# Gated DeltaNet and routed experts on one core: modulation moved to TensorE, the triangular inverse in blocks of 16 rows, and a planner with other durations

## The chip, the core and the metric

The kernel runs on one core of a Trainium2 chip. The metric is the time of one execution on the device in microseconds (us). Five engines work side by side, each in the fixed order of its own queue: TensorE (PE in the profile, its weight loads PEld), VectorE (DVE), ScalarE (ACT), GpSimd (POOL) and SyncE (SP), which here does nothing but issue DMAs. An instruction that waits holds up all that stands behind it on its engine.

## The reference, cut to what matters

One layer of depth, 512 latent tokens and 256 context tokens of width 1024. First the six modulation vectors (`mod`), a normalised and modulated input, the bidirectional gated DeltaNet with 8 heads of 128, then 16 experts of which each takes 64 tokens.

```python
mod = c_act @ w_mod[i] + b_mod[i]            # 1024 -> 6 * 1024: sh_m, sc_m, gt_m, sh_f, sc_f, gt_f
u = modulate(rmsnorm(h, norm_mix_g[i]), sh_m, sc_m)
...
# in gated_deltanet, for each direction, head and chunk
a_low = where(strict, einsum('bhnid,bhnjd->bhnij', k_beta, k) * decay, 0.0)
lmat = a_low + eye(CHUNK)
sol = triangular_solve(lmat, rhs, lower=True, unit_diagonal=True)
...
def step(S, inp):                            # scan over chunks
    v_new = u_n - w_n @ S
    o_n = qd_n @ S + att_n @ v_new
    S = S * gt_n + kt_n.T @ v_new
...
h = h + gt_m * y
h = h + gt_f * ec_moe(modulate(rmsnorm(h, norm_ffn_g[i]), sh_f, sc_f), ...)
```

## The kernel before, in words

**Two stages.** The first is the token mixer: norms, modulation, projections, eight heads, output projection, router. The second runs the 16 experts and reads some 400 MB of expert weights through a ring of buffers; its first weights are fetched (`prefetch`, `fetch`) while the mixer ends.

**The mixer per head.** `bulk` (L400 on) projects v, q, k and z with the split input (`proj_step`, L141 to L143: three matmuls a step, eight steps an item, 31 items in all, those of k and v also for the context). `conv` runs the short convolution on DVE and ACT. Then each head goes through:
- `head_a` (L1050 on): decay matrices `ff`, read by a broadcasting DMA from `grow_d` and masked on POOL; k times k on PE (L1114); the product `ct`, of which the diagonal blocks go into `cd` and by DMA to `bd` in DRAM.
- `invert` (L1130 on): `lb` is read back so that 96 partitions hold 48 blocks of 32 rows, each twice, for the even and the odd columns of the inverse. POOL then works forward substitution, 31 steps of a product (`tb`, L1148) and a subtraction (`xb`, L1150). The result goes out to `xd` and comes back as `cr`.
- `head_b` (L1208 on): the blocks of 32 are merged to 64 and to 128 on PE, with copies and transposes on DVE and ACT between, into `XT`.
- `scan` (L1304 on): both directions over 6 chunks, each with a chain of PE, DVE, PE, ACT, PE, DVE; needs `XT` and the scan of the head before. `head_o` (L1358 on) normalises the output, which the tail multiplies with the output weights (L457 to L459).

**The modulation for later.** `mods` (L337 on) loads 32 pieces of the modulation weights, 128 columns each, into two slots (`e<-in_wm`). `mod_piece` weights each of the 8 slabs of 128 rows with the activation and adds them: on DVE in 8 steps (L373, L375), or on POOL or ACT with a tree of additions, by a letter for each piece in the table `MOD_E`. One small matmul with ones then sums over partitions (L382, L396), and DVE adds it into its place.

**What sets the order.** All five queues of the mixer come from a planner inside the program (`run`, L205 on). Each step is written as a generator that asks for an engine and a duration (`Ask("P", 0.67, ...)`); the planner plays them against a clock of its own with ranks (scans first, projections last), a delay `HOP` after each engine, a model of the DMA (`dma`), and rings of buffers, and the instructions are written in the order in which steps start there. On the chip the queues keep that order; only the waits are real. Names with a trailing number are tiles of the heads (`ck`, `cv`, `e`, `ua`, `wa`, `ya` hold k, v, XT and others in turn).

Of the kernel before, what the change touches and what calls it, by code (L numbers as in the profile page):

```python
# [11 lines left out]
F32 = mybir.dt.float32  # L12
F32R = mybir.dt.float32r
AF = mybir.ActivationFunctionType
OP = mybir.AluOpType
# [4 lines left out]
P = 128  # L20
D = 1024
# [18 lines left out]
NB = 2 * NCH * 4  # L40
# [9 lines left out]
def gdn_moe_kernel(ctx: ExitStack, tc: tile.TileContext, a, out):  # L50
# [3 lines left out]
    def psum_tile(pool, shape, tag, bufs, name=None):  # L54
# [9 lines left out]
    par = const.tile([2 * NB, 2], F32)  # L64
    g.affine_select(out=par[:, 0:1], in_=ones[:2 * NB, 0:1], pattern=[[0, 1]], compare_op=OP.is_ge, fill=0.0,
                    base=NB - 1, channel_multiplier=-1)
    g.affine_select(out=par[:, 1:2], in_=ones[:2 * NB, 0:1], pattern=[[0, 1]], compare_op=OP.is_ge, fill=0.0,
                    base=-NB, channel_multiplier=1)
# [7 lines left out]
    v.tensor_add(selr, selr, ident[:, 96:])  # L76
    epsc = const.tile([P, 3], F32)
# [71 lines left out]
    HOP = {"P": 0.27, "A": 0.33, "V": 0.33, "G": 0.35, "D": 0.0, None: 0.0}  # L149
    PRE = 1  # L150
    E_AT = (410, 425)
    EARLY_G = 4
    MOD_STEP = 7
    MOD_E = "GGAGVVVVGVBVAVAVVVVVAVGAVVVVBVGV"
# [5 lines left out]
    def dma(nbytes, at=0.0):  # L160

        dq[0] = max(dq[0], at + 0.7) + nbytes / 360e3
        return dq[0] + 1.1
# [75 lines left out]
    av = lambda n_: 0.1 + n_ * 0.00084  # L239
    dv = lambda n_: 0.08 + n_ * 0.00104  # L240
# [17 lines left out]
    def conv(nm, h, n_, parts, last):  # L258
# [8 lines left out]
        else:  # L267
# [10 lines left out]
            for j in range(5):  # L278
                t = yield Ask("VA"[j == 0], 1.06 * dv(w) if j else 1.11 * av(w), t)
                if j == 0:  # L280
                    s.mul(t_, pad[:, o:o + w], taps[:, 0:1])
                else:
                    v.scalar_tensor_tensor(t_, pad[:, o + j:o + j + w], taps[:, j:j + 1], t_, op0=OP.mult, op1=OP.add)
# [63 lines left out]
    def mod_piece(n_, j, wm, wsl, t):  # L347

        t = yield Ask(None, 0.0, lambda: t if n_ < 2 else None if ("mm", n_ - 2) not in done else max(t, done["mm", n_ - 2]))
        if MOD_E[n_] != "V":  # L350
            if MOD_E[n_] == "G":
                for i in range(2):
                    t = yield Ask("G", 1.25, t)
                    hk = slice(4 * i, 4 * i + 4)
                    g.tensor_tensor(wm[:, hk], wm[:, hk], cs1[:, hk, 0:1].to_broadcast([P, 4, P]), OP.mult)
            else:
                for i in range(4):
                    t = yield Ask("A", 0.59, t)
                    for k in (2 * i, 2 * i + 1):
                        s.mul(wm[:, k], wm[:, k], cs1[:, k, 0:1])  # L360
            en, on = ("V", v) if MOD_E[n_] == "B" else ("G", g)
            for i in (4, 2):
                t = yield Ask(en, dv(P * i) if en == "V" else 0.25 + 0.27 * i, t)
                on.tensor_add(wm[:, :i], wm[:, :i], wm[:, i:2 * i])
            t = yield Ask(en, dv(P) if en == "V" else 0.5, t)
            acc = accs[n_ % 2]
            on.tensor_add(acc, wm[:, 0], wm[:, 1])
        else:
            acc = accs[n_ % 2]
            for k in range(KT):  # L370
                t = yield Ask("V", 0.25, t)
                if k == 0:
                    v.tensor_scalar(acc, wm[:, k], cs1[:, k, 0:1], None, op0=OP.mult)  # L373
                else:
                    v.scalar_tensor_tensor(acc, wm[:, k], cs1[:, k, 0:1], acc, op0=OP.mult, op1=OP.add)  # L375
        give(wsl, t + 1.0)
        b1 = slice(16 + j, 17 + j)
        t = yield Ask("P", 0.15, t + 3.0, "pq")
        sl = take("pq")
        if 8 <= j < 24:  # L380
            pc = psum_tile(ps, [P, 1], "pq", 3)
            pe.matmul(pc, acc, ones[:, 0:1], start=True, stop=True)  # L382
            k1 = slice(j % 8, j % 8 + 1)
            t = yield Ask("V", 0.15, t)
# [1366 lines left out]
```

## Time and profile before

| | us |
|---|---|
| median of 3 runs | 1574.02 (1568.37 to 1576.02) |
| profiled execution, its own time | 1573.24 |
| its span in the profile | 1571.5 |
| mixer, until the first expert matmuls | 0 to about 634 |
| experts | about 634 to 1571.5 |

Busy times over the span are PE 87%, DVE 46%, ACT 26%, POOL 24%; but the share of an engine that works in one stage alone says little, so the profile is read by stretches. A row of a view of stretches gives the length and then, for each engine, busy time and number of instructions, the granted TensorE clock as a share of full speed, the share of the DMA engines and their GB/s. A busy PE counts the modelled length of overlapping matmuls: what a matmul really takes from the queue is read from the distance between two starts.

### The profile page before, as it was taken

Reading aid. Unit: us, or ns where it says so; the run is one execution under the profiler, and the core shown is the slowest. Engines: PE = TensorE matmul, PEld = TensorE weight load, DVE = VectorE, ACT = ScalarE, POOL = GpSimd, SP = SyncE. Lnnn points to the kernel's source line nnn. Section 1 sums busy time; section 2 is a strip of 40 time slices with the busy share of each in tenths; the row PEclk is TensorE's granted clock in tenths of the full one; section 3 lists DMA queues with packets and bytes.
Section 4 is the critical chain, followed back from the end, with each engine's and each line's share of the span. In section 5 each row is a group of like instructions: output and inputs, shape, how many; then the busy total and the mean of one; then the engine's idle time right before and its main releaser. Section 6 shows DMA issues by size and latency. Waiting matters only on the chain.

```text
span 1571.5 us, 20699 instructions
## 1 busy us (share of the span) xinstructions
PE 1374.7 (87%) x8058; PEld 752.6 (48%) x8058; DVE 721.5 (46%) x1545; ACT 405.3 (26%) x1038; POOL 381.0 (24%) x645
## 2 busy tenths in 40 slices
PE   5889898988986889999999989889889899899867
PEld 1677687766875766433434324224223323324314
DVE  7779896977995896222222222222222222222103
ACT  3356474655574533000000000000000000000012
POOL 2548866857657830000000000000000000000001
PEclk8889999999998999999999999999999999999979
DMA  8145443443453566899999999999999999999992
GB/s 347 54 135 142 135 114 91 117 130 95 133 122 72 205 243 248 364 426 426 425 426 425 425 426 426 427 425 425 426 425 426 426 425 426 425 426 426 425 426 109
DMA packets 112515, 480.12 MB, mean 306 GB/s; under 512 B 45505, under 2 KB 66209, under 8 KB 81826
## 3 DMA queue, kind: packets, MB, share of 16 engines
q1 hardware_dynamic: 112418, 478.81, 77.9%
q8 instruction: 63, 1.03, 0.3%
q14 instruction: 34, 0.28, 0.1%
HBM read 471.92 MB, written 6.86 MB: 305 GB/s over the span
## 4 chain that ended last, share of the span: by engine, by line
DMA 48%; PE 26%; DVE 14%; POOL 8%; issue 2%; ACT 1%; SPq 0%; DVEq 0%; POOLq 0%; ACTq 0%
DMA w<-in_wgu 25%; DMA w<-in_wd 13%; PE gu L1580 10%; PE dn L1561 4%; POOL xb L1150 3%; POOL tb L1148 3%; DMA cr<-xd 2%; DVE e L375 2%; PE gc L1561 2%; PE gc L1511 2%; DMA fg<-in_fg 1%; DVE wl L303 1%; DMA ff__690<-grow_d 1%; DMA ff__1139<-grow_d 1%; PE gc L1548 1%
## 5 line engine op out<-in xcount | busy, mean ns | idle before, releaser
L1580 PE MATMUL gu<-w,xsT 128*64 128x512 f32 x2044 | 472.9, 606 | 32.4 <-DMA w<-in_wgu 31.6
L1580 PEld LDWEIGHTS gu<-w,xsT 128*64 128x64 f32 x2044 | 138.4, 138 | 291.5 <-issue 239.4
L1667 POOL TENSOR_TENSOR hres<-acc,fg 128x256 f32<-128x256 f32 (+1 forms) x6 | 6.0, 1004 | 953.1 <-DVE acc L1655 953.0
L1561 PE MATMUL dn<-w,work 128*64 128x512 f32 x896 | 202.0, 600 | 25.2 <-DMA w<-in_wd 25.2
L1550 DVE TENSOR_TENSOR acc<-gc,acc 128x512 f32<-128x512 f32 x104 | 70.7, 690 | 299.5 <-PE gc L1548 299.5
L141 PE MATMUL pp<-uh,wh 128*128 128x512 f32 (+1 forms) x368 | 153.4, 417 | 1.7 <-ACT cz L265 1.7
L143 PE MATMUL pp<-uh,wl 128*128 128x512 f32 (+1 forms) x368 | 138.9, 377 | 3.8 <-DVE wl L303 2.9
L142 PE MATMUL pp<-ul,wh 128*128 128x512 f32 (+1 forms) x368 | 137.9, 375 | 0.0
L1561 PEld LDWEIGHTS dn<-w,work 128*64 128x64 f32 x896 | 62.4, 137 | 154.2 <-issue 116.8
L1148 POOL TENSOR_TENSOR tb<-lb,xb 96x126 f32<-96x126 f32 (+22 forms) x248 | 118.3, 477 | 65.8 <-DMA lb<-bd 48.6
L1150 POOL TENSOR_TENSOR xb<-xb,tb 96x126 f32<-96x126 f32 (+22 forms) x248 | 125.1, 504 | 19.4
L1532 ACT ACTIVATE work<-tr 128x512 f32<-128x512 f32 x14 | 8.4, 597 | 423.1 <-PE tr L1525 423.1
L1512 DVE TENSOR_SCALAR xsT<-gc,ffn 128x128 f32<-128x128 f32 x64 | 26.2, 410 | 154.1 <-PE gc L1511 154.1
L1542 ACT CAST yh<-work 64x512 fp32r<-64x512 f32 x28 | 17.3, 617 | 253.1 <-DVE work L1539 252.8
L143 PEld LDWEIGHTS pp<-uh,wl 128*128 128x128 f32 x368 | 74.7, 203 | 16.1 <-DVE wl L303 3.3
L141 PEld LDWEIGHTS pp<-uh,wh 128*128 128x128 f32 x368 | 75.1, 204 | 10.7 <-ACT cz L265 2.2
L142 PEld LDWEIGHTS pp<-ul,wh 128*128 128x128 f32 x368 | 75.3, 205 | 6.3
L1511 PEld LDWEIGHTS gc<-oneh,hres 128*128 128x128 f32 x512 | 64.5, 191 | 20.2 <-issue 18.3
L1511 PE MATMUL gc<-oneh,hres 128*128 128x128 f32 x512 | 69.2, 280 | 0.4 <-DVE oneh L1504 0.4
L375 DVE SCALAR_TENSOR_TENSOR e<-e,cs,e 128x128 f32<-128x128 f32 x133 | 66.0, 512 | 1.8
L1613 DVE TENSOR_TENSOR work<-gu,work 128x512 f32<-128x512 f32 x32 | 22.0, 692 | 80.9 <-PE gu L1580 79.7
L1548 PEld LDWEIGHTS gc<-yh,pgt 128*128 128x128 f32 x112 | 19.8, 186 | 82.0 <-issue 68.2
(443 smaller groups left out, 2042.7 us busy)
## 6 DMA issues: line engine op xcount, KB each, us to landing
w<-in_wgu SPq DMA_DIRECT2D x100, 2048.0 KB, 34.3
w<-in_wd SPq DMA_DIRECT2D x45, 2048.0 KB, 34.3
w<-in_wgu SPq DMA_DIRECT2D x55, 1024.0 KB, 31.9
w<-in_wd SPq DMA_DIRECT2D x22, 1024.0 KB, 31.8
e<-in_wm SPq DMA_DIRECT2D x32, 512.0 KB, 4.4
wt<-in_win SPq DMA_DIRECT2D x31, 512.0 KB, 4.6
w<-in_wdt SPq DMA_DIRECT2D x6, 2048.0 KB, 30.7
wm<-in_wm SPq DMA_DIRECT2D x3, 2048.0 KB, 14.6
```

The lines of the kernel that those rows point to most:

```text
L141: pe.matmul(pp, wh[:, k, :], uh[i][:, k, :], start=k == 0, stop=False)
L142: pe.matmul(pp, wh[:, k, :], ul[i][:, k, :], start=False, stop=False)
L143: pe.matmul(pp, wl[:, k, :], uh[i][:, k, :], start=False, stop=k == KT - 1)
L375: v.scalar_tensor_tensor(acc, wm[:, k], cs1[:, k, 0:1], acc, op0=OP.mult, op1=OP.add)
L1148: g.tensor_tensor(t_, lb[:, k + 1:, k:k + 1].to_broadcast([2 * NB, m, n_]), xb[:, k:k + 1, 0:n_].to_broadcast([2 * NB, m, n_]), OP.mult)
L1150: g.tensor_tensor(xb[:, k + 1:, 0:n_], xb[:, k + 1:, 0:n_], t_, OP.subtract)
L1511: pe.matmul(pg, hres[:, t, k * P:k * P + P], oneh[:, t].rearrange("p a b -> p (a b)"), start=t == 0, stop=t == NC_LAT - 1)
L1512: v.tensor_scalar(xsT[:, k, :], pg, ffn[:, 0, k:k + 1], ffn[:, 1, k:k + 1], op0=OP.mult, op1=OP.add)
L1548: pe.matmul(pcb, pgt[:, t, :], yh[:, dh], start=True, stop=True)
L1550: v.tensor_add(acc[t // 2][:, t % 2, cs], pcb, hres[:, t, cs] if first else acc[t // 2][:, t % 2, cs])
L1561: pe.matmul(pd[64 * g_:64 * g_ + 64], hs_[g_][i][:, cb, 64 * j:64 * j + 64], wcols(w, c0, w_), start=ft == 0, stop=ft == 15, tile_position ...
L1580: pe.matmul(gu[m][f // 2][hs], xsT[:, k, es], wcols(w, 2048 * m + 512 * f, 512), start=k == 0, stop=k == KT - 1, tile_position=(0, 64 * (f ...
```

## The change

It has three parts, and the planner then writes all queues of the mixer anew.

1. **Modulation on PE.** `mod_piece` no longer weights and adds on DVE, POOL or ACT, and the table `MOD_E` is gone. Eight matmuls with the activation as 32 columns of weights (`cst`, mostly zeros) sum over the partitions into four strips of one PSUM tile; ACT copies it, and the matmul that was there already now takes `sel` or `selb` in place of ones. The loads stand further apart (`MOD_STEP` 11 instead of 7).
2. **Blocks of 16.** `head_a` packs the diagonal blocks of 16 (`c16`, with two masks `hm`). `invert` has 96 blocks of 16 rows on 96 partitions, 15 steps instead of 31, and the three transfers carry half as many bytes or less. `head_b` gets one more merge, from 16 to 32, ahead of the others: 2 x 48 tiny matmuls with a product on ACT, two transposes and a subtraction on DVE. `cd` is kept for it.
3. **Numbers of the planner.** The durations of nearly all steps, `HOP`, `E_AT` (the earliest planned start of the first two expert loads) and `dma` (a later landing for broadcasts) are other numbers.

```diff
-    HOP = {"P": 0.27, "A": 0.33, "V": 0.33, "G": 0.35, "D": 0.0, None: 0.0}
+    HOP = {"P": 0.22, "A": 0.06, "V": 0.06, "G": 0.08, "D": 0.0, None: 0.0}
-    MOD_E = "GGAGVVVVGVBVAVAVVVVVAVGAVVVVBVGV"
...
     def mod_piece(n_, j, wm, wsl, t):
-            for k in range(KT):
-                t = yield Ask("V", 0.25, t)
-                    v.scalar_tensor_tensor(acc, wm[:, k], cs1[:, k, 0:1], acc, op0=OP.mult, op1=OP.add)
...
+        pm = psum_tile(ps, [P, P], "pq", 3)
+        for k in range(KT):
+            q = 32 * (k % 4)
+            pe.matmul(pm[q:q + 32, :], cst[:, k, :], wm[:, k, :], start=k < 4, stop=k >= 4)
+        t = yield Ask("A", 0.27, t)
+        s.copy(acc, pm)
...
     def invert(h, bd, tl_):
-        for k in range(31):
-            m, n_ = 31 - k, k // 2 + 1
+        for k in range(15):
+            m, n_ = 15 - k, k + 1
             g.tensor_tensor(t_, lb[:, k + 1:, k:k + 1]..., xb[:, k:k + 1, 0:n_]..., OP.mult)
             g.tensor_tensor(xb[:, k + 1:, 0:n_], xb[:, k + 1:, 0:n_], t_, OP.subtract)
...
     def head_b(h):
+        s.mul(lo[:, :, :, 16:], x["cr"], hm[:, 1:2])
+        v.tensor_scalar(lo[:, :, :, :16], x["cr"], hm[:, 0:1], None, op0=OP.mult)
+        # 48 matmuls, 32 x 16, of x["cd"] with lo
+        v.transpose(flat(up), flat(lo))
+        s.mul(y1, py, hm[:, 1:2])
+        # 48 matmuls, 32 x 16, of up with y1
+        v.tensor_sub(lo[:, :, :, :16], lo[:, :, :, :16], pu)
+        v.transpose(flat(up), flat(lo))
```

Where it moves instructions, three places. First SP, where it serves the inverse of head 6 before (`xd_5226` is its result, `bd_5234` belongs to head 7, `wt` are projection weights, `ff` and `qa` broadcasts, `od` a head's output):

```order
L1060 DMA ff__5000<-grow_d 128x6x128
L136 DMA wt<-in_win 128x1024
L1153 DMA xd_5226<-xb 96x512
L1128 DMA bd_5234<-cd 128x12x32
L136 DMA wt<-in_win 128x1024
L1290 DMA qa<-grow_d 128x4x128 x2
L1158 DMA cr<-xd_5226 128x24x16
L1137 DMA lb<-bd_5234 48x1024 x2
```

The same service in the changed program, for the head whose transfers are numbered 4641 and 4908:

```order
L1113 DMA bd_4641<-c_4638 128x12x16
L341 DMA e_451<-in_wm 128x1024
L134 DMA wt<-in_win 128x1024
L1121 DMA lb<-bd_4641 96x256
L1404 DMA od_4731<-cz 128x512
L1042 DMA ff__4779<-grow_d 128x6x128
L134 DMA wt<-in_win 128x1024
L341 DMA e_451<-in_wm 128x1024
L1042 DMA ff__4874<-grow_d 128x6x128
L1136 DMA xd_4908<-xb 96x256
L134 DMA wt<-in_win 128x1024
L1141 DMA cr<-xd_4908 128x12x16
```

Before, the next head's `bd` and two more transfers stand between a head's `xd` and its `cr`. Now a head's `lb`, `xd` and `cr` follow each other among loads, and the next head's `bd` stands behind its `cr`.

Second, PE where the merge of head 6 begins before (`cx` are the inverted blocks, `ct` the matrix, `pp` projections, `ident` transposes):

```order
L143 MATMUL pp<-uh_110,wl 128x512
L1227 MATMUL pq<-cx,ct 32x32 x24
L141 MATMUL pp<-uh_110,wh 128x512
L142 MATMUL pp<-ul_112,wh 128x512
L143 MATMUL pp<-uh_110,wl 128x512
L1042 MATMUL pq<-ident,cv 128x128 x4
L1237 MATMUL pq<-yb,cx 32x32 x24
```

The same place in the changed program, where the last projections stand 23 rows above:

```order
L1211 MATMUL pq<-cx,cd 32x16 x48
L1332 MATMUL sc_5800<-R,ua 128x128
L1359 MATMUL po<-wa,qa 128x128
L1363 MATMUL po<-vx,ya 128x128
L1096 MATMUL pq<-ya 128x128 x6
L1224 MATMUL pq<-y_5894,cx 32x16 x48
L1155 MATMUL pq<-wa,ya 128x128 x4
L1024 MATMUL pq<-ident,cv 128x128 x6
L1024 MATMUL pq<-ident,wa 128x128 x4
L1238 MATMUL pq<-cx,ct 32x32 x24
L1248 MATMUL pq<-yb,cx 32x32 x24
```

Before, projections filled the merge of head 6, and the k times k of head 7 (L1114) stood ahead of it; now the projections are all done one scan earlier, the merge of head 6 begins inside the scan of head 5, and the k times k of head 7 (L1096) stands in the middle of it with no projection left.

## Rows read from the trace of the kernel before

**Rows 1.** Stretch of the experts: length, engines, granted clock, DMA share, GB/s.
```profile
core 0: us, PE busy (x) PEld busy (x) DVE busy (x) ACT busy (x) POOL busy (x), PEclk, DMA share, GB/s
640.00:1545.00 905.00, 821.62 (x3838) 308.65 (x3835) 203.34 (x401) 62.91 (x115) 0.00 (x0) 0.98 1.00 422
```

**Rows 2.** Chain that ended last, from 60 to 640 us, by line.
```profile
by line: POOL xb L1150 9.3%; POOL tb L1148 8.4%; DMA cr<-xd 5.5%; DVE e L375 5.4%; issue 5.3%; DVE wl L303 2.5%; DMA ff__690<-grow_d 2.5%; DMA ff__1139<-grow_d 2.4%; DMA ff__3654<-grow_d 2.3%; DMA e<-in_wm 1.9%; DMA xd<-xb 1.9%; DMA ff__237
```

**Rows 3.** SP's waits, 100 to 560 us: total, times, longest.
```profile
SPq L1153 <- POOL xb L1150: 99.4, 7, 28.9
```

**Rows 4.** Stretches of scans and between scans, in turn, then to the experts.
```profile
181.00:215.00 34.00, 29.69 (x241) 25.21 (x240) 30.94 (x84) 22.31 (x62) 22.36 (x43) 1.00 0.43 123
215.00:229.00 14.00, 12.61 (x148) 9.86 (x147) 13.64 (x27) 12.90 (x43) 9.38 (x18) 1.00 0.36 103
229.00:261.00 32.00, 30.29 (x191) 26.59 (x190) 24.84 (x60) 15.55 (x51) 25.66 (x46) 0.95 0.19 50
261.00:287.00 26.00, 19.53 (x220) 15.21 (x220) 17.12 (x45) 16.93 (x46) 15.05 (x36) 0.87 0.66 165
287.00:324.00 37.00, 33.67 (x248) 28.08 (x249) 34.03 (x81) 18.69 (x56) 26.07 (x45) 0.95 0.53 123
324.00:346.00 22.00, 16.43 (x160) 12.79 (x159) 15.57 (x33) 14.14 (x37) 16.76 (x34) 0.85 0.40 138
346.00:384.00 38.00, 30.73 (x242) 26.94 (x241) 25.04 (x62) 19.21 (x61) 23.16 (x42) 0.95 0.30 77
...
485.00:521.00 36.00, 21.67 (x227) 17.02 (x226) 20.84 (x37) 16.68 (x47) 25.41 (x45) 0.81 0.44 94
521.00:544.00 23.00, 20.27 (x131) 17.17 (x130) 19.11 (x43) 10.59 (x25) 19.61 (x27) 1.00 0.77 275
544.00:574.00 30.00, 26.08 (x243) 20.25 (x242) 26.11 (x49) 12.80 (x31) 14.67 (x25) 1.00 0.60 179
574.00:601.00 27.00, 25.78 (x194) 22.03 (x194) 22.06 (x54) 7.32 (x18) 4.42 (x3) 1.00 0.80 325
601.00:634.00 33.00, 30.36 (x169) 18.29 (x169) 22.11 (x66) 13.09 (x35) 0.24 (x1) 1.00 0.54 198
```

**Rows 5.** Page, costliest groups: substitution and modulation steps; busy, mean ns, idle before.
```profile
L1148 POOL TENSOR_TENSOR tb<-lb,xb 96x126 f32<-96x126 f32 (+22 forms) x248 | 118.3, 477 | 65.8 <-DMA lb<-bd 48.6
L1150 POOL TENSOR_TENSOR xb<-xb,tb 96x126 f32<-96x126 f32 (+22 forms) x248 | 125.1, 504 | 19.4
L375 DVE SCALAR_TENSOR_TENSOR e<-e,cs,e 128x128 f32<-128x128 f32 x133 | 66.0, 512 | 1.8
```

**Rows 6.** Groups by form on POOL, 40 to 640 us: short substitution steps.
```profile
L1148 POOL TENSOR_TENSOR tb<-lb,xb 96x56 f32<-96x56 f32 x16 | 7.1, 444 | 1.2
...
L1150 POOL TENSOR_TENSOR xb<-xb,tb 96x30 f32<-96x30 f32 x16 | 5.8, 361 | 1.3
```

**Rows 7.** PE in order of time: start, us, line, tiles, records merged.
```profile
84.00 0.39 PE L141 MATMUL pp<-uh,wh 128*128 128x512 f32 x1
...
84.68 0.39 PE L141 MATMUL pp<-uh,wh 128*128 128x512 f32 x1
...
505.60 0.98 PE L1227 MATMUL pq<-cx,ct 32*32 32x32 f32 x48 [8.46 <-DVE cx L1218]
...
599.00 0.64 PE L514 MATMUL pq<-hT,wr 128*32 128x128 f32 x16
599.58 0.49 PE L1321 MATMUL sc<-R,ua 128*128 128x128 f32 x2
599.82 0.47 PE L457 MATMUL pp<-woh,oh 128*128 128x512 f32 x1
```

**Rows 8.** DVE in order of time, inside the merge of head 6.
```profile
513.43 4.10 DVE L1266 COPY e<-cx 32x192 f32<-32x192 f32 x4
```

**Rows 9.** Page, DMA issues: KB each, median us from issue to landing.
```profile
e<-in_wm SPq DMA_DIRECT2D x32, 512.0 KB, 4.4
```

## The prediction on record

> **What bounds the kernel now.** I read the stretches first. From 640 to 1545 us the DMA engines are busy at a share of 1.00 and move 422 GB/s [rows 1]: the experts wait for their weights, in an order that the change doesn't touch. The ring is filled before they start, so their 937 us from 634 to the end of the span follow the mixer as a block, and a mixer that ends one us earlier gives one us. All that is to be found is when the experts start.
>
> In the mixer no engine is full. The chain from 60 to 640 us names POOL's substitution first, 9.3% and 8.4% of 580 us, that is 103 us, then its transfers, `cr` 5.5% and `xd` 1.9%, 43 us, and DVE's modulation step 5.4%, 31 us [rows 2]. SP tells the same in another way: it stood 99.4 us in all, up to 28.9 at a time, before `xd` until POOL had finished [rows 3], and what stood behind it, projection weights among it, was not issued in that time.
>
> The third view cuts the mixer at its scans [rows 4]. The eight scans take 34, 32, 37, 38, 29, 28, 23 and 27 us, 248 in all, the seven stretches between them 14, 26, 22, 15, 29, 36 and 30, 172 in all (four rows are left out); the first scan starts at 181, and after the last come 33 us of output projection, router and top-k. The reader is to see the stretch before scan 6: 36 us, PE busy 21.67, and in it PE idle 8.46 us before the merge's first matmuls, for `cx` [rows 4, 7].
>
> **What PE has to do, stretch by stretch.** I counted the matmuls that stand in each stretch of PE's order and priced them by distances of starts: a projection step of three is 0.68 (84.00 to 84.68), a matmul of two records and 128 columns 0.24 (599.58 to 599.82; I take 0.22, since the second waits a little), eight tiled matmuls of 32 x 128 0.58 with what follows them (I take 0.44), and 24 tiny ones below 0.98, of which the last one's way is part; I take 0.03 each [rows 7]. Before, the scans hold 26, 27, 29, 27, 24, 26, 18 and 24 us of PE work, 200, and the stretches between 11, 15, 13, 11, 21, 18 and 25, 113. So a us of work took 248/200 = 1.24 us in scans, but 172/113 = 1.52 between them: there PE waits for the inverse and the merge. In the new order the scans hold 30, 29, 25, 25, 26, 23, 21 and 22, 199, and the stretches between 19, 25, 28, 21, 19, 7 and 18, 138. The added 25 us between scans are projections that stood elsewhere, modulation and the new merge.
>
> **The change part by part.** *Substitution.* Before, 62 POOL steps a head take (118.3 + 125.1)/8 = 30.4 us [rows 5], with POOL's modulation steps between them. After, 30 steps with 15 to 64 elements: those of 56 and 30 took 444 and 361 ns [rows 6], so 0.4 x 30 = 12 us, bounds 11 and 14. That takes 18 us a head out of POOL and out of the way from `ct` to `cr`, and SP's wait before `xd` falls with it. The transfers keep their fixed way; for half the bytes I count nothing, bounds 0 and 2 us a head.
>
> *The new merge.* On DVE it replaces four copies and two transposes by a product, two transposes, a subtraction and the packing of `c16`. On the path it adds two rounds of 48 tiny matmuls (48 x 0.03 = 1.4 us each), a product on ACT, a subtraction and a transpose, some 4 us; a merge takes some 16 before (first matmuls at 505.60, scan 6 at 521 [rows 4, 7]), so about 20. In the order it begins inside the scan before it, and the inverse that it waits for is 18 us shorter, so the 4 us are covered; uncovered they cost 7 x 4 = 28 us. For PE it is 8 x 2.9 = 23 us, in the counts above.
>
> *Modulation.* DVE loses 133 steps, 66.0 us [rows 5], of 80 to 90% busy stretches such as 181 to 215 (30.94 of 34) [rows 4]; POOL and ACT lose their pieces. PE gains 32 x 0.44 = 14 us, ACT 32 short copies. PE now stands before a piece whose weights have not landed, and behind it every scan and projection: the landing takes 4.4 us in the median [rows 9]. SP issues a load as soon as its slot is free, one piece ahead, so I count 0. It can't be below that, for PE did none of this before; at the other end, if a quarter of the pieces wait for a whole landing, 8 x 4.4 = 35 us.
>
> *The planner.* Between scans I put PE's work at 1.15 us for each us, near the 1.14 of the last scan (27 against 24), in which DVE and POOL were light [rows 4], and no stretch under 16, the merge less what lies in the scan: 22 + 29 + 32 + 24 + 22 + 16 + 21 = 166 (bounds 1.05 and 1.3). Scans at 1.10, but none under 24, since the chain alone took 23 in scan 6: 33 + 32 + 28 + 27 + 29 + 25 + 24 + 24 = 222 (bounds 1.05 and 1.24). The first scan stands behind 136 us of PE work instead of 130, but its inverse is 18 us shorter, and DVE lighter by five of the first ten pieces (`V` in the table), 5 x 8 x 0.5 = 20 us: 168 instead of 181 (bounds 160 and 181). After the last scan more is left: in the order five tiles of the router instead of two and twice the output projections, 7.6 us of PE work, so 42 instead of 33 (bounds 36 and 48).
>
> **The sum.** 168 + 222 + 166 + 42 = 598 us instead of 634: 36 us. The profiled execution took 1573.24, span 1571.5 and 1.7 around it, so 1573.2 - 36 = 1537. It is 0.8 under the median of 1574.02, which is far inside the three runs' spread.
>
> **A rule beside it.** In the merge of head 6 four copies of 32 x 192 took 4.10 us [rows 8], 1.03 each, while POOL worked 25.41 of the 36 us [rows 4]. The Trainium skill (SBUF — State Buffer, Who interferes with whom) says that DVE's copies in a two-port mode and its operations with two inputs in SBUF share ports with GpSimd, and that the second to issue is blocked in full. The trace agrees with it as far as the modulation step goes, which took 512 ns in the mean [rows 5] for 128 elements. By the rule a POOL that works half as long gives DVE's copies back some 1 us a head on the path, and the sum would be 8 us less, 1529. I don't count it, as the scans' ratio takes part of it in.
>
> **The rivals.** *A, more:* what PE waited for is gone altogether, and only the merge and PE's own work are left: scans and stretches at 1.05, 213 + 150, first scan at 163, 38 after: 564, that is 70 us less, 1503. For it: POOL and DVE fall so far that PE alone is left; against it: a scan's chain with little else took 23 us for 18 of work.
>
> *B, slower:* the ratios belong to PE's fixed queue and not to POOL. Each merge is a chain of small steps on PE, DVE and ACT, longer by one round now; if what stands between them is planned with too short delays (`HOP` after DVE and ACT 0.06), PE stands before each, and the 138 us between scans take 1.52 as before, the scans 1.24: 181 + 247 + 210 + 42 = 680, 46 us more, 1619. It decides from a ratio of 1.46 between scans on, with the other terms as forecast (168 + 222 + 42 + 138 x 1.46 = 634). For it: the stretches of PE's queue are full of waits already; against it: the longest of them end on `cx`, that is on POOL and `cr`.
>
> *C, nothing:* modulation on PE gives it all back: a quarter of the pieces hold PE for a landing, 35 us as above, and the time stays at 1572. For it: landings are late when broadcasts are under way; against it: loads are issued a piece ahead.
>
> **How the numbers follow.** Forecast 1537 with a chance of 0.62, A 0.18, B 0.09, C 0.11. The forecast's own bounds taken half way together reach from 1510 to 1566; A adds the part down to 1500, C the part up to 1568. Left out are B, what of A lies below, and half of C: under 2 in 10. About 0.5%, 8 us, is what a measurement here can tell from no change. Forecast and A are faster by more than that but for a little: 0.79; C and that little are the same: 0.11; B and the worse part of C are slower: 0.10.
>
> **What would show it.** SP's wait before `xd` falls from 99.4 to under 50 us; POOL's steps a head from 30 to about 12; the stretches between scans sum to about 166 at 138 us of PE work; the first scan starts near 168, the experts near 598; the experts' part stays 937. PE idle before the eight matmuls of a piece, for its weights, over 10 us in all would speak for C; stretches between scans over 200 us, ended by DVE and ACT, for B. The step that I trust least is the ratio of 1.15.

## The result: slower by 1.5%, where 2.3% faster was forecast

The changed kernel takes 1596.49 us in the median (1591.21 to 1600.80), the kernel before, beside it, 1572.95 (1568.37 to 1576.02): a ratio of 1.0151 with an interval of 1.0109 to 1.0192. The profiled execution took 1594.72 us with a span of 1592.9. The forecast was 1537, with a range from 1500 to 1568.

The experts behave as forecast: their first matmul on the weights `w` (tile `gu`) starts at 656.59 us, and from there to the end of the span it is 936.3 us (before 635.75 and 935.8). So the whole loss, 21 us, is a mixer that ends later, and the question is only why.

The first part of the page of the changed kernel gives busy time, share of the span and instructions of each engine; before, PE had 1374.7 us in 8058, DVE 721.5, POOL 381.0.

```profile
PE 1415.7 (89%) x10106; PEld 784.6 (49%) x10106; DVE 647.1 (41%) x1390; ACT 405.0 (25%) x1032; POOL 188.7 (12%) x342
```

POOL has lost half of its work and DVE a tenth, as meant; PE has gained 41 us. Cut at its scans as in [rows 4], the changed kernel looks like this (columns as in [rows 1]: PE, PEld, DVE, ACT and POOL busy, granted clock, DMA share, GB/s; scans and stretches between them in turn, seven rows left out):

```profile
174.00:205.00 31.00, 30.84 (x412) 27.52 (x413) 20.15 (x54) 14.47 (x48) 3.25 (x5) 1.00 0.37 97
205.00:230.00 25.00, 21.31 (x257) 17.51 (x256) 20.16 (x40) 18.94 (x44) 13.52 (x32) 1.00 0.47 130
230.00:262.00 32.00, 31.88 (x419) 28.03 (x419) 20.64 (x52) 15.68 (x47) 3.67 (x5) 0.95 0.36 111
...
439.00:470.00 31.00, 25.65 (x456) 20.78 (x457) 21.85 (x44) 21.67 (x55) 12.86 (x31) 0.78 0.33 89
470.00:498.00 28.00, 26.39 (x261) 22.51 (x260) 13.21 (x42) 13.41 (x41) 9.12 (x12) 0.93 0.66 195
498.00:516.00 18.00, 10.71 (x270) 9.22 (x268) 15.61 (x34) 13.90 (x46) 7.90 (x12) 0.69 0.30 63
...
544.00:570.00 26.00, 20.34 (x394) 15.61 (x394) 15.09 (x35) 11.28 (x33) 4.98 (x4) 0.92 0.46 116
570.00:599.00 29.00, 28.25 (x143) 23.44 (x144) 18.14 (x44) 6.65 (x15) 6.30 (x5) 0.84 0.81 316
599.00:656.00 57.00, 46.31 (x247) 28.77 (x246) 31.48 (x86) 14.88 (x39) 0.27 (x1) 0.88 0.34 128
```

The scans take 31, 32, 30, 32, 30, 28, 28 and 29 us, 240 in all (before 248); the stretches between them 25, 30, 30, 25, 31, 18 and 26, 185 (before 172); the first scan starts at 174 (181), the last ends at 599 (601), and after it come 57 us where there were 34. So the mixer's chain gained 2 us up to the last scan and lost 23 behind it. The reader is to see the PE column in the scans: 30.84 of 31, 31.88 of 32, 28.25 of 29, and 229 of the 240 us of all eight. DVE and POOL have room there now, and PE has next to none.

The waits that the prediction named did shrink. SP stands 55.2 us before the transfer of `xb` to DRAM (99.4 in [rows 3]), and the substitution's 30 steps of a head take (52.7 + 45.0)/8 = 12.2 us instead of 30.4 [rows 5]. SP's wait, and POOL's two costliest groups up to the experts (busy, mean ns, idle before):

```profile
SPq L1136 <- POOL xb L1133: 55.2, 8, 14.4
```

```profile
L1131 POOL TENSOR_TENSOR tb<-lb,xb 96x15 f32<-96x15 f32 (+7 forms) x120 | 52.7, 439 | 70.9 <-DMA lb<-bd 62.3
L1133 POOL TENSOR_TENSOR xb<-xb,tb 96x15 f32<-96x15 f32 (+7 forms) x120 | 45.0, 375 | 9.4
```

The first of the two groups shows what came in place: POOL, done sooner, waits 62.3 us for the block's transfer `lb` (48.6 in [rows 5]). PE's costliest wait went too. It stood before the first matmuls of a merge, for `cx`; here is the row of the kernel before and then that of the changed one, 100 to 620 us (us in all, times, longest):

```profile
PE pq L1227 <- DVE cx L1218: 19.6, 5, 8.5
```

```profile
PE pq L1211 <- DVE cx L1203: 2.2, 2, 2.0
```

In the tail, PE in order of time (start, us, line, tiles, records merged, idle time before and what ended it):

```profile
627.02 0.64 PE L494 MATMUL pq<-hT,wr 128*32 128x128 f32 x16 [0.59 <-ACT hT L519]
632.67 0.61 PE L504 MATMUL pq<-selr,rs 128*128 128x16 f32 x2 [5.01 <-ACT rs L499]
633.55 1.89 PE L558 MATMUL pq<-w,ot 128*128 128x16 f32 x8 [0.27 <-DVE w L507]
635.28 6.39 PE L1440 MATMUL pp<-hres,ident 128*128 128x512 f32 x8
```

Router tiles and output projections that stood before or inside the last scan are now behind it (PE busy 46.31 us in the tail, 30.36 in [rows 4]). PE stands idle for 5.01 us while ScalarE works off squares and a copy in its own order, and then the 8 matmuls that only keep TensorE busy take 6.39 us; in the kernel before, the same 8 took 3.68 and were done before the top-k needed PE.

### The profile page after: what moved, and what is told of

Read it like the earlier page. It is cut to its first block, busy times and chain, and to the rows that moved or that the text cites. A ratio compares the mean times of both kernels' runs of the same rounds, so it can differ in the third digit from the quotient of the medians.

```text
span 1592.9 us, 24355 instructions
## 1 busy us (share of the span) xinstructions
PE 1415.7 (89%) x10106; PEld 784.6 (49%) x10106; DVE 647.1 (41%) x1390; ACT 405.0 (25%) x1032; POOL 188.7 (12%) x342
## 4 chain that ended last, share of the span: by engine, by line
PE 45%; DMA 40%; DVE 8%; ACT 3%; issue 2%; POOL 1%; DVEq 0%; SPq 0%; ACTq 0%; POOLq 0%
DMA w<-in_wgu 25%; DMA w<-in_wd 12%; PE gu L1591 10%; PE pp L139 4%; PE dn L1572 3%; PE pp L140 3%; PE pp L141 3%; PE gc L1572 2%; PE sc L1332 2%; PE gc L1522 2%; PE sc L1344 1%; DMA fg<-in_fg 1%; PE sc L1326 1%; PE pp L437 1%; PE pp L438 1%
## 5 line engine op out<-in xcount | busy, mean ns | idle before, releaser
L139 PE MATMUL pp<-uh,wh 128*128 128x512 f32 (+1 forms) x368 | 149.6, 407 | 1.9 <-ACT pad L270 1.8
L141 PE MATMUL pp<-uh,wl 128*128 128x512 f32 (+1 forms) x368 | 134.8, 366 | 1.7 <-POOL wl L300 1.7
L1131 POOL TENSOR_TENSOR tb<-lb,xb 96x15 f32<-96x15 f32 (+7 forms) x120 | 52.7, 439 | 70.9 <-DMA lb<-bd 62.3
L1559 PE MATMUL gc<-yh,pgt 128*128 128x512 f32 x112 | 52.3, 487 | 7.7 <-DVE acc L1561 7.7
L1337 ACT ACTIVATE Vs<-sc,vsc 128x128 f32<-128x128 f32 x80 | 28.0, 366 | 102.4 <-PE sc L1332 100.9
```

The lines of the kernel that those rows point to most:

```text
L139: pe.matmul(pp, wh[:, k, :], uh[i][:, k, :], start=k == 0, stop=False)
L141: pe.matmul(pp, wl[:, k, :], uh[i][:, k, :], start=False, stop=k == KT - 1)
L1131: g.tensor_tensor(t_, lb[:, k + 1:, k:k + 1].to_broadcast([NB, m, n_]), xb[:, k:k + 1, 0:n_].to_broadcast([NB, m, n_]), OP.mult)
L1337: s.mul(Vs, pv, x["vsc"][:, d, c:c + 1])
L1559: pe.matmul(pcb, pgt[:, t, :], yh[:, dh], start=True, stop=True)
```

## The experiments

First a view that all of them share. PE's busy time from the start of the span to the first matmul of the experts, one row each of the kernel before, of the changed one, and of the two runs that turned out to matter most (e5: relief without the new matmuls; e17: both parts of the change in the order of before).

```profile
0.00:635.75 635.75, 533.11 (x4014) 429.27 (x4014) 505.34 (x1117) 334.94 (x898) 374.99 (x639) 0.92 0.50 148
```

```profile
0.00:656.59 656.59, 575.23 (x6063) 461.74 (x6063) 430.75 (x962) 334.62 (x892) 182.72 (x336) 0.92 0.45 137
```

```profile
0.00:576.13 576.13, 512.57 (x4014) 419.40 (x4015) 439.14 (x999) 320.85 (x849) 232.17 (x371) 0.96 0.53 164
```

```profile
0.00:631.87 631.87, 557.92 (x6062) 449.61 (x6062) 420.69 (x962) 330.79 (x890) 181.37 (x336) 0.94 0.47 142
```

The experts' start is PE busy plus PE idle: 533 + 103 before, 575 + 81 in the changed kernel. The change took 21 us of idle time from PE and gave it 42 us more of busy time. The other runs in the same form (us; ratio to the kernel before with its 95% interval; the last column is the time behind the last scan):

| run | time | ratio | experts start | PE busy | PE idle | tail |
|---|---|---|---|---|---|---|
| changed kernel | 1596.5 | 1.0109 to 1.0192 | 656.6 | 575 | 81 | 57 |
| e1 both parts, old numbers | 1597.1 | 1.0122 to 1.0187 | 658.9 | 568 | 91 | 70 |
| e2 modulation alone | 1588.8 | 1.0066 to 1.0121 | 651.8 | 553 | 98 | 34 |
| e3 blocks of 16 alone | 1594.5 | 1.0094 to 1.0165 | 656.0 | 557 | 99 | 44 |
| e4 full matmul lengths | 1587.5 | 1.0051 to 1.0110 | 651.0 | 566 | 85 | 40 |
| e5 relief without matmuls | 1515.7 | 0.9616 to 0.9645 | 576.1 | 513 | 64 | 35 |
| e6 modulation matmuls twice | 1605.2 | 1.0188 to 1.0221 | 666.2 | 583 | 83 | 56 |
| e7 before, waits 0.30 | 1585.5 | 1.0061 to 1.0095 | 646.3 | 539 | 108 | 35 |
| e8 both parts, experts later | 1592.5 | 1.0097 to 1.0140 | 655.0 | 564 | 91 | 58 |
| e9 modulation, old order | 1569.2 | 0.9927 to 0.9971 | 633.1 | 543 | 90 | 34 |
| e10 relief of substitution | 1542.6 | 0.9757 to 0.9821 | 606.4 | 522 | 85 | 34 |
| e11 half the new matmuls | 1575.8 | 0.9988 to 1.0028 | 636.2 | 553 | 83 | 56 |
| e12 changed, old waits | 1569.2 | 0.9947 to 0.9978 | 630.2 | 564 | 66 | 49 |
| e13 waits 0.20 | 1596.6 | 1.0143 to 1.0183 | 659.8 | 570 | 90 | 54 |
| e14 waits 0.30 | 1585.5 | 1.0071 to 1.0118 | 647.4 | 568 | 79 | 55 |
| e15 waits 0.42 | 1574.8 | 1.0004 to 1.0026 | 637.5 | 562 | 76 | 53 |
| e16 full lengths, waits 0.33 | 1612.3 | 1.0221 to 1.0292 | 677.1 | 574 | 104 | 56 |
| e17 both parts, old order | 1569.7 | 0.9964 to 1.0001 | 631.9 | 558 | 74 | 34 |
| e18 blocks of 16, old order | 1577.4 | 1.0008 to 1.0044 | 639.4 | 546 | 94 | 34 |

### Which part? e1 to e4

The first theory was that the new numbers of the planner spoil a good change (N), the rival that the new work on TensorE costs more than the relief gives (W).

e1 takes the code of both parts and puts the numbers back, all but `MOD_STEP` and the durations of steps that only the new code has:

```
-    HOP = {"P": 0.22, "A": 0.06, "V": 0.06, "G": 0.08, "D": 0.0, None: 0.0}
-    E_AT = (440, 460)
+    HOP = {"P": 0.27, "A": 0.33, "V": 0.33, "G": 0.35, "D": 0.0, None: 0.0}
+    E_AT = (410, 425)
...
-                    t = yield Ask("P", (0.69, 0.355)[i], both, None if k else "pp")
+                    t = yield Ask("P", (0.67, 0.36)[i], both, None if k else "pp")
```

> The kernel before with both parts of the code changed (modulation on TensorE, substitution on blocks of 16 with the third merge) and the planner's numbers left as they were before (waits between engines 0.33, matmuls of 128 f32 columns at 0.225, projections 0.67, modulation and merge steps that both versions have at their old durations). Theory N (the new numbers are the cause): the two parts by themselves pay, so this stands below the kernel before, 1540 to 1568 us, with the tail after the last scan near 35 us and the scans below 235 us in all. Theory W (the new work on TensorE is the cause, modulation or merges): it stands near the changed kernel, 1585 to 1605 us, whatever the planner counts.

1597.13 us. The old numbers save nothing: N falls in its simple form. The split is another, though: the last scan ends at 589 us, 12 before that of the kernel before, and then come 70 us of tail. On the chain there stands a load that was slow to land (start, us, what), which e8 was made for:

```profile
597.59 11.10 DMA wot<-in_wo
```

e2 is the kernel before with `mod_piece` of the changed one, its constants and its `MOD_STEP`; e3 is the kernel before with `invert`, the start of `head_b` and the packing of `c16` of the changed one.

```
-            for k in range(KT):
-                t = yield Ask("V", 0.25, t)
...
+            pe.matmul(pm[q:q + 32, :], cst[:, k, :], wm[:, k, :], start=k < 4, stop=k >= 4)
```

> The kernel before with only the modulation moved to TensorE; substitution on 32 rows and the planner's numbers as before. Theory N: near or below the kernel before, 1550 to 1575 us. Theory W in its form 'modulation': slower than before by most of what the whole change loses, 1585 to 1600 us, because the 32 groups of 8 tiled matmuls take 14 us of TensorE's queue and wait for their loads ahead of the heads' matmuls. Theory W in its form 'merges': 1560 to 1575 us.

1588.78 us, as W in its form "modulation" has it.

```
-        for k in range(31):
-            m, n_ = 31 - k, k // 2 + 1
+        for k in range(15):
+            m, n_ = 15 - k, k + 1
```

> The kernel before with only the substitution on blocks of 16 and its additional merge on TensorE; modulation on VectorE and GpSimd and the planner's numbers as before. Theory N: near or below the kernel before, 1550 to 1575 us, with the wait of the gathering transfer for the substitution below 60 us. Theory W in its form 'merges': 1585 to 1600 us, since the inversion's chain got two TensorE rounds longer. Theory W in its form 'modulation': 1555 to 1575 us.

1594.54 us, as W in its form "merges" has it. Each part alone loses, 14 and 20 us, and together they lose 23. That speaks for W, but the sum doesn't add up, and e2 and e3 also have lists of their own.

e4 is the changed kernel with the matmuls counted in the plan at the length that they have in the trace, such as

```
-            t = yield Ask("P", 0.11, t, f"sc{d}")
+            t = yield Ask("P", 0.22, t, f"sc{d}")
```

> The changed kernel with one kind of number in the planner's list changed: f32 matmuls are counted with the time that they hold TensorE in the trace (0.22 us for 128 columns and not 0.11, so 0.22 and 0.44 in the scan, 0.88 for the four of q, 1.1 and 1.0 for the merges' rounds, 0.5 for the 8 tiled ones of a modulation). Waits between engines stay at the new 0.06. Theory N in its form 'TensorE counted too short': most of the loss returns, 1555 to 1578 us, tail after the last scan below 45 us. Theory N in its form 'waits between engines counted too short': little changes, 1588 to 1600 us. Theory W: 1588 to 1605 us.

1587.48 us, 9 less than the changed kernel and between the theories.

### What are relief and price worth when the order is held? e5, e6, e10, e11

These four change no place in PE's order: the planner counts the same, only work is left out or doubled (so the results of e5, e10 and e11 are not the reference's). Two theories stand against each other: P, that PE's own queue bounds the mixer and relief elsewhere is worth little, and R, that the relief is worth what the prediction took and the new matmuls eat it. e5 leaves out every second step of the substitution, and of each modulation all but one or two of the products and most of the additions; the transfers keep their size:

```
             t = yield Ask("G", 0.41 + m * n_ * 0.0044, tl_)
+            if k % 2:
+                continue
...
+                if k > 1:
+                    continue
```

> The kernel before in its own order of instructions, with work left out on GpSimd, VectorE and ScalarE and nothing put on TensorE: every second step of the substitution, and of each modulation's 8 products all but one or two (so its results are not the reference's). This is the relief that the change gives, without its price. Theory P (TensorE's own queue bounds the mixer; what it waits for elsewhere is mostly replaced by the next wait): 1560 to 1573 us, that is at most 15 us of gain. Theory R (the relief is worth what the prediction took for it, and the new matmuls eat it): 1525 to 1545 us.

1515.67 us, 58 us less than before: theory R, and more than it asked for. The relief is real; P in the form "relief is worth little" falls. In the row above, PE's idle time falls from 103 to 64 us, and its busy time from 533 to 513 for the same 4014 records, at a mean granted clock of 0.96 instead of 0.92.

e10 has the first of these two edits alone:

```
             t = yield Ask("G", 0.41 + m * n_ * 0.0044, tl_)
+            if k % 2:
+                continue
```

> The kernel before in its own order, with only every second step of the substitution on GpSimd left out (so its results are not the reference's); all modulations stay. With both reliefs the time was 1515.7 us, 58 us less than before. If the substitution carries most of it (GpSimd is then free for the gathering transfer and the modulations on it): 1520 to 1540 us. If the modulations on VectorE carry it: 1555 to 1570 us. Both alike: 1540 to 1555 us.

1542.57 us: 31 us of the 58 are the substitution's; the rest, 27, is what the modulations add to it.

The price, at the changed kernel's order:

```
-        for k in range(KT):
+        for k in (*range(KT), *range(KT)):
             q = 32 * (k % 4)
             pe.matmul(pm[q:q + 32, :], cst[:, k, :], wm[:, k, :], start=k < 4, stop=k >= 4)
```

> The changed kernel, same order, with the 8 tiled matmuls of each of the 32 modulations done twice (256 more matmuls, 32 groups; a group holds TensorE for 0.57 us in the trace of the changed kernel, so some 18 us of work). Theory P: most of it comes through, 1608 to 1615 us. If TensorE had room (its idle 81 us before the first expert matmul taken up): 1596 to 1602 us.

1605.21 us, 8.7 more than the changed kernel. A group of 16 tiled matmuls holds PE 1.01 us in the median, one of 8 0.57, so 32 x 0.44 = 14 us were added, and 0.6 of each came through.

```
-        for k in range(KT):
+        for k in range(4):
...
-                    pe.matmul(py[R[b], d, c, :], x["cd"][R[b], 1 - d, c, :], lo[R[b], d, c, :16], start=True, stop=True, tile_position=(32 * b, 32 * b))
+        pe.matmul(py, ident, lo[:, :, :, :16], start=True, stop=True)
```

> The changed kernel in its own order with less of its new TensorE work: 4 of the 8 tiled matmuls of a modulation, and for each of the two rounds of the new merge one matmul of 192 columns for 48 small ones (so its results are not the reference's); some 17 us less of TensorE's time by the lengths in the trace (0.57 us for 8, 0.92 us for 48). Theory P: nearly all of it comes out, 1578 to 1582 us. Theory O: half of it or less, as in the run with the matmuls twice (+8.7 us for 18 us of work): 1586 to 1594 us.

1575.79 us, 20.7 less. A modulation's group now holds PE 0.36 us and a round of the merge 0.36 instead of 0.92 and 1.02, so some 7 and 10 us were taken out, and all came out of the time. So each us of PE's new work costs 0.6 to 1.2 us of the time. Both factors are rough, for the changed kernel's own interval is 6 us to either side; but by e11 the work is not hidden behind waits.

### How much is the order? e7, e8, e9, e17, e18

```
-    HOP = {"P": 0.27, "A": 0.33, "V": 0.33, "G": 0.35, "D": 0.0, None: 0.0}
+    HOP = {"P": 0.27, "A": 0.30, "V": 0.30, "G": 0.32, "D": 0.0, None: 0.0}
```

> The kernel before with one harmless change of the planner: the wait after ScalarE, VectorE and GpSimd counted at 0.30, 0.30 and 0.32 us and not 0.33, 0.33 and 0.35. No work is added or left out. It says how far the time moves by the order alone. If the order matters little: 1567 to 1580 us. If the list of before is a good draw among many (theory O: any other list costs 10 us or more by the place where the last projections fall): 1583 to 1600 us.

1585.54 us: 12 us for a change that adds and removes nothing. Theory O, that the order of before is a good draw, got its first support.

```
-    E_AT = (410, 425)
+    E_AT = (440, 460)
```

> The kernel of the first run of the study (both parts, numbers of before; 1597 us, last scan ended at 589 us, but the first expert matmul began at 659) with one number changed: the first loads of expert weights may start at 440 and 460 of the planner's time and not at 410 and 425. In that run the last output-projection weights took 11 us to land among the expert weights. Theory D (the tail got long because the early expert weights hold up the projection's loads): 1570 to 1585 us, tail 40 to 55 us. Theory P (TensorE's work was only pushed behind the last scan): 1588 to 1600 us, tail plus scans unchanged in sum.

1592.51 us, 5 less than e1; the tail is 12 shorter and the last scan ends 8 later. The load behind the experts' weights is a small part; most of the tail is work that was pushed there.

e9 does the modulation on PE, but lets the planner go on counting the old steps, and issues the 8 matmuls and the copy where the first and second old product stood. All rows of before stand in their old sequence on PE, with the 32 new groups put between.

```
             for k in range(KT):
                 t = yield Ask("V", 0.25, t)
+                part(k // 3 if k % 3 == 0 else -1)
```

> Modulation on TensorE as in the changed kernel, but in the order of before: the planner still counts the old modulation steps, so every other instruction of every engine stands where it stood, and the 8 tiled matmuls and the copy stand where the first and the second of the old products stood. The second run of the study had the same work in an order planned anew: 1588.8 us. Theory O (the order that a new list gives is the cause): 1545 to 1568 us, below the kernel before, since the relief of VectorE and GpSimd stays and 18 us of tiled matmuls come in at about half price. Theory P (the matmuls themselves are the cause): 1578 to 1592 us, as in the second run.

1569.18 us. The same work took 1588.78 in the order that the planner made for it (e2): 20 us are the order's. Against the kernel before it gains 0.5%, a little less than theory O asked for and just at what can be told from no change.

e17 does the same for both parts: the substitution counts its old 31 steps and issues 15, and the new merge takes no time in the plan (e18 has this without the modulation).

```
+        for k in range(31):
+            m, n_ = 31 - k, k // 2 + 1
+            t = yield Ask("G", 0.41 + m * n_ * 0.0044, tl_)
+            if k > 14:
+                continue
...
-        t1 = yield Ask("P", 0.66, t, "pq")
+        yield Ask(None, 0.0, lambda: None if fin(("I", h)) is None else fin(("I", h)) - 2.2)
```

> Both parts of the changed code in the order of before: the planner counts the old modulations and the old substitution, the new instructions stand where the old ones stood, and the new merge's 16 rounds lie 3 to 6 us ahead of the old merges, with 6 to 12 matmuls between its two rounds. TensorE's rows of before all stand in their old sequence. Relief 58 us (as in the run that left the work out) less 33 us for the new matmuls at their traced lengths (18 for the modulations, 15 for the merges) is 25 us below before. Theory O (order is what the change lost by): 1545 to 1562 us. Theory P (the work itself does not pay): 1573 to 1595 us.

1569.66 us, ratio 0.9964 to 1.0001: neither theory's number. The same code in a new list took 1597 (e1), so 27 us are the order's; but with the order held the change gives nothing either. The 58 us of relief are used up. The rows of e5 and e17 above say where: in e17 PE is busy for 45 us more than in e5 (557.92 against 512.57) and idle for 10 us more. The new matmuls cover 40 of e17's busy us; the old ones alone cover 523 there and 513 in e5, at a mean granted clock of 0.94 and 0.96, and some of both overlap. So four fifths of the relief went into PE's busy time, and one fifth into waits. The largest waits that are left: PE waits for the new merge's input, DVE behind it for the transfer `cr`, and POOL for `lb` (engine, line, releaser: us in all, times, longest).

```profile
PE pq L1234 <- DVE cx L1227: 18.3, 6, 8.1
...
DVE cx L1227 <- DMA cr<-xd: 25.8, 6, 7.7
...
POOL tb L1155 <- DMA lb<-bd: 96.4, 6, 19.7
```

The first row is nearly the 19.6 us of the kernel before. The substitution is some 18 us a head shorter, but the way from the landing of `lb` to that of `cr` takes 44 us in the mean of seven heads, where it took 50: SP serves it in the old order. That doesn't tell e17 from e5, where it takes 43. And in the changed kernel's own order it takes 27 us (six heads), without any gain in the time. So a shorter way of the inverse, from which the prediction took its main gain, doesn't by itself make these versions faster.

> Blocks of 16 with the new merge alone, in the order of before in the same way; modulations as before. In a new order this part gave 1594.5 us. Relief of the substitution alone was worth 31 us with half of its steps left out; the new merge's matmuls take 15. Theory O: 1552 to 1566 us. Theory P: 1573 to 1595 us.

1577.43 us, as theory P has it: 17 less than in a new order (e3), and 0.1 to 0.4% above before. This part by itself doesn't pay, in the old order either: a like relief was worth 31 us (e10), and all of it is spent.

### Is it one number? e12 to e16

e12 is the changed kernel with only `HOP` put back.

```
-    HOP = {"P": 0.22, "A": 0.06, "V": 0.06, "G": 0.08, "D": 0.0, None: 0.0}
+    HOP = {"P": 0.27, "A": 0.33, "V": 0.33, "G": 0.35, "D": 0.0, None: 0.0}
```

> The changed kernel with one line of the planner's numbers put back: the waits after an engine at 0.27, 0.33, 0.33 and 0.35 us as before and not 0.22, 0.06, 0.06 and 0.08. Theory H (the short waits make TensorE's queue stand at the scans' hand-overs, the prediction's rival B): 1565 to 1580 us. Theory O (this is one more order among many): 1585 to 1602 us.

1569.18 us, 27 less than the changed kernel: this looked like the rival B of the prediction and its short `HOP` (theory H). But e1, with the same `HOP` and the other numbers old as well, had 1597. So three of the next four runs moved `HOP` alone, and the fourth corrected the lengths as well.

```
-    HOP = {"P": 0.22, "A": 0.06, "V": 0.06, "G": 0.08, "D": 0.0, None: 0.0}
+    HOP = {"P": 0.27, "A": 0.20, "V": 0.20, "G": 0.22, "D": 0.0, None: 0.0}
```

> The changed kernel, waits after ScalarE, VectorE and GpSimd counted at 0.20, 0.20 and 0.22 us (TensorE 0.27). At 0.06 the time was 1596 us, at 0.33 it was 1569. Theory H (short waits are the cause, steadily): 1576 to 1586 us. Theory O (every list a draw, scatter of 10 to 30 us): anywhere from 1565 to 1605, no order along the series 0.06, 0.20, 0.30, 0.33, 0.42.

The same with 0.30 (e14) and 0.42 (e15):

> The changed kernel, waits counted at 0.30, 0.30 and 0.32 us (TensorE 0.27), next to the 0.33 that gave 1569 us. Theory H: 1566 to 1576 us. Theory O: a neighbour is no nearer than others, so more than 8 us from 1569 is likely (on the kernel before, the same step of 0.03 cost 12 us).

> The changed kernel, waits counted at 0.42, 0.42 and 0.44 us (TensorE 0.27). The traces show 0.6 to 0.85 us from the end of a VectorE step over a TensorE round to the next start, where 0.33 and 0.27 plan for about 0.83. Theory H: flat or better behind 0.33, 1560 to 1572 us. Theory O: as scattered as the others.

e16 has the `HOP` of e12 and the lengths of e4, such as

```
-            t = yield Ask("P", 0.11, t, f"sc{d}")
+            t = yield Ask("P", 0.22, t, f"sc{d}")
```

> The changed kernel with both corrections: f32 matmuls counted at the time for which they hold TensorE (as in the fourth run, 1587.5 us with waits of 0.06) and the waits of before (0.33, as in the run that gave 1569). Theory H: the two add up, 1555 to 1566 us. Theory O: 1565 to 1600 us.

With 0.06, 0.20, 0.30, 0.33 and 0.42 the times are 1596.5, 1596.6, 1585.5, 1569.2 and 1574.8. The three longest waits are better than the two shortest, but a step of 0.03 makes 16 us, and with better lengths, which alone had helped by 9 (e4), the wait of 0.33 gives the worst time of all, 1612.3. That is theory O: the nine lists for the same work lie between 1569 and 1612 us, and no one of the numbers settles where. That waits of 0.3 and more are better in the mean is likely, and not shown.

## Why the prediction was wrong, point by point

**The experts' block.** Right: it was to stay as it is, and from the first matmul on `gu` to the end it took 935.8 us before and 936.3 after. Every run moved by as much as its experts' start.

**The relief.** Right in kind and too small. POOL's steps of a head went to 12.2 us (12 forecast), SP's wait to 55 (under 50 forecast), the modulation left DVE. By e5, a like relief is worth 58 us without its price. The forecast gained 36 net, with 25 us more work on PE between the scans. DVE's copies in the merge also got shorter, as the rule beside the sum had it. By form, before and after (busy, mean ns):

```profile
L1266 DVE COPY e<-cx 32x192 f32<-32x192 f32 x16 | 10.1, 633 | 0.2
```

```profile
L1277 DVE COPY e<-cx 32x192 f32<-32x192 f32 x16 | 5.5, 342 | 0.2
```

They fell from 633 to 342 ns with POOL's work halved. Those of this form (with the other target, `ua`, 32 in each kernel) during which POOL did nothing took 252 ns before and 249 after, the others 615 and 377. The Trainium skill's rule (SBUF — State Buffer, Who interferes with whom), that DVE's copies in a two-port mode share ports with GpSimd, agrees with these numbers. The time gained did not reach the end.

**The new work on PE.** Its size was right: 14 + 23 = 37 us were counted, the medians give 32 x 0.57 = 18 and 16 x 0.92 = 15. Its effect was not: the merge's part was taken for covered on the path, and by e6 and e11 each us of the new work costs 0.6 to 1.2 us of the whole.

**The ratios of 1.10 and 1.15: the step that failed.** Scans and stretches between them were forecast at 222 + 166 = 388 us for 337 us of work. Measured are 240 + 185 = 425, that is ratios of 1.21 and 1.34. PE's busy time alone, summed over these 15 stretches, is 228.8 + 159.0 = 388 us. So the forecast left PE not one us of idle time. The rows of before could have told it: there the same stretches hold 359 us of PE busy for 313 us of work, 1.15, and the rest, 61 us, idle. (The printed terms of these counts sum to 1 or 2 us more or less than their totals; no reading hangs on it.) What I read as a ratio with a little waiting left in it was the ratio without any: a us of counted work took 1.15 us of busy PE before (359 for 313) and after (388 for 337). Stretches at the lower granted clock have a part in it; the parts were not measured. The last scan, which I took for the measure, had 25.78 us busy of 27 [rows 4]: a stretch nearly without idle time. In truth idle time fell from 61 to 37 us, and busy time rose by 28. That is 37 of the 58 us by which the forecast missed.

**First scan and tail.** 168 forecast, 174 measured: 6 us, whose cause is open. The tail, 42 forecast with bounds to 48, took 57. Some 2 of these 15 us are a matter of the mark: the forecast counts from 634, and the first matmul on `gu` stood at 635.75 before. For the others the trace shows the 8 matmuls at 6.39 instead of 3.68 us, ScalarE's squares, of which four pairs of 1.16 us stand on the chain where one pair stood, and more projections and router behind the last scan; these were not priced one by one. 37 + 6 + 15 = 58, from 1537 to the 1594.7 of the profiled execution.

**The planner's list.** No term of the sum had it, and it is as large as the effect itself. e2, e3 and e1 against e9, e18 and e17: the same work, 20, 17 and 27 us apart by the order alone, and 12 us by a nudge on the kernel before (e7). The prediction took a count of work in the new order for the whole of what an order does. Held in the old order, the change gives 0 to 0.4% (e17); the loss of 1.5% is the order's, and the missing gain went for four fifths into PE's busy time (e17 against e5).

**The rivals.** C didn't happen: PE waited 1.0 us for the weights of a piece. A didn't. B came nearest, as the only one that was slower, but not by its mechanism: PE's waits in the scans and between them shrank, from 61 to 37 us, the ratios (1.21 and 1.34) stayed under B's 1.24 and 1.52, and its cause, the short `HOP`, is one of several numbers that draw another order. What makes one order better than the next is open: PE's idle time ranges from 66 us (e12) to 104 (e16) for the same work, and no stretch or line holds the whole difference.

No version that does the whole work beats the kernel before by much: by their intervals e9 and e12 lie 0.2 to 0.7% below it and e17 0 to 0.4%, at the edge of what can be told from no change.

## What to carry to other kernels

Before a forecast lets waits vanish, compare it with the busy time of the engine that everything passes: a sum that equals that busy time has no wait left in it, and new work on that engine has little to hide behind (here each us of it cost 0.6 to 1.2 us). Where a planner makes the order, run the new work once in the old order and the old work once in a nudged list: here the first separated 0 from 23 us, and the second showed 12 us of scatter that no cause explains. And a gain seen with work left out (58 us) is not the forecast of a change: here the engine to which the work was moved took 45 us of it back.

## What the runs showed of the hardware

Fewer waits on TensorE went with a higher clock, and the same matmuls then took less time. In e5 the same 4014 records up to the experts took 512.6 us busy where the kernel before needed 533.1, at a mean granted clock of 0.96 against 0.92. Of the two levels, 1.2 and 2.4 GHz, the lower one was granted for 51 of 576 us in e5 and for 96 of 636 before, and PE was busy in 43 and 73 us of that. If work takes twice as long at the lower level, the 31 us less are worth some 15 (an estimate from these numbers), that is most of the 20 us of busy time, and a quarter of e5's 58. In the changed kernel the clock was 0.69 in the mean of the stretch from 498 to 516 us, in which PE was busy for 10.71 of 18 us with small matmuls and waits, and 0.58 from 634 to 642, behind the idle 5 us of the tail; there the eight matmuls of 512 columns took 0.80 us each, and 0.46 in the kernel before.

```profile
634.00:642.00 8.00, 8.00 (x20) 4.29 (x21) 1.74 (x8) 0.26 (x1) 0.00 (x0) 0.58 0.00 0
```
